# A two-layer encoder kernel: four modulation dots moved into attention, the first gate strip fetched between the value weights, and seven smaller edits of the order

## The chip, the cores and the metric

The kernel runs on one NeuronCore of a Trainium2 chip. The metric is the device time of one execution in microseconds, as the median of a few runs; lower is better. The core has a matrix engine (TensorE, in the profile PE, its weight loads PEld) and four others: VectorE (DVE), ScalarE (ACT), GpSimd (POOL) and SyncE (SP). Each engine works through its own list of instructions in order, and waits on semaphores where an instruction needs what another engine or a transfer has not delivered. In this kernel all transfers are issued by SP, so they form one more list that is worked through in order ("SPq").

## The reference

1024 tokens of width 1024 pass through two layers. Each layer is a root-mean-square norm with a shift and a scale that come from a conditioning vector c, a token mixer, a SiLU gate, an output projection and a gated residual add; a last norm closes the trunk.

```python
def _modulation(c, ada_w, ada_b):
    mod = jax.nn.silu(c) @ ada_w + ada_b
    shift, scale, gate = jnp.split(mod[:, None, :], 3, axis=-1)

for i in range(DEPTH):                                  # two layers
    shift, scale, gate = _modulation(c, ada_w[i], ada_b[i])
    h = _rmsnorm(x, norm_g[i]) * (1.0 + scale) + shift
    y = _diff_attention(h, ...) if i == 0 else _mla(h, ...)
    x = x + gate * y
return _rmsnorm(x, final_norm_g)

def _diff_attention(...):                               # layer 0, 8 heads, q and k of 2 x 64, v of 128
    q, k, v, z = jnp.split(h @ w_in, ...)               # rope on q and k
    p = jax.nn.softmax(sc, axis=-1)
    p = p[:, :, 0] - lam * p[:, :, 1]                   # difference of two softmaxes
    o = _rmsnorm(p @ v, subln_g) * (1.0 - lambda_init)
    return (o * jax.nn.silu(z)) @ w_out
```

Layer 1 is multi-head latent attention: one input projection to a low-rank query, a latent key/value, one rope key and the gate, then expansion to 8 heads, softmax, and the same gate and output projection.

## The kernel before, in words

**Precision.** Every large product is made of three matmuls on a high and a low part (`mm3`, L182 to L184: high·high, high·low, low·high). A part is made by a cast on ACT (high) and a subtraction on DVE or POOL (low). PE therefore has some 7,350 matmuls in one fixed order, and the program is a question of having the parts ready in time.

**Layer 0, first pass.** The tokens are taken in two halves of 512. For each of eight blocks of 128 features `h_chunk` transposes the tokens (L468), scales and shifts them (high part on ACT L473, the full value on DVE L477 or ACT L475) and subtracts (L478). With them PE makes the values of the first four heads (`vacc`), and, from weight strips, the keys and queries of head 0 (`acc`). A strip is 1024 x 128 weights for one head and one of k, q and z (z is the gate's input): two loads of 256 KB into `wraw` (L206, two buffers), a cast (L227), a subtraction (L228).

**V phase.** Then follow eight tiles `vps` of 28 or more matmuls (`v0_tile`): the values of the other four heads, one tile of 128 tokens each, from eight row blocks of weights `wv1[k]`. A block is loaded into `wvr` (L524, two buffers), cast (L533, ACT) and subtracted (L534, DVE); the subtraction is what frees the buffer for the next load. The first three blocks (`WV1` = 3) are loaded early, the other five behind `store_v`'s last cast. The first gate strip `z0raw` is fetched and used after the tiles have begun. Between the tiles run the streamed strips of the next heads and rope (transfers `rp_sw` L323).

**Modulation dots.** Layer 1's shift and scale need 16 dots `mod_dot` (L424, DVE, 128 x 1024): each needs a block of 512 KB that `mod_load` fetches (L419) and multiplies it with silu(c), with the sum along each row. Six stand in the second half of the first pass (k = 1 to 6), ten in the V phase (`MODS` = 2, 3, 3, 2 per tile). Layer 0's gate has eight more, made during attention 0 by `gate_steps0`, a generator that takes one step per query tile: load ahead, two steps, dot, two steps, dot.

**Attention 0.** For each head and query tile: scores (L850), row maximum (L400 DVE), exponential (L402 ACT), the two softmaxes combined (`e`, L858 DVE), four transposes (L383), a cast (`pth` L385 ACT) and a subtraction (`ptl` L386 DVE), the product with the values. A list of side tasks (`side`) is moved on by one entry at each tick; strips, rope, stacking of q (`qa`, `qb`, L352 to L358) and the row scales `bc_s` (L410) hang on it. The last head's task list of q holds as many empty ticks as the others'.

**Output projection.** `Seven` and `Pre7` make it of seven half-size products instead of eight. `Pre7` does the first products inside attention 0 and copies its sums out of the accumulators (`done`, L1264) when the next product begins.

**Transition.** The last products are added to the residual (`add0`, L1398), `group0` normalises four token tiles (reciprocal root on POOL L169, scaling of x on DVE L457 and ACT L455, tiles 1 and 3 on ACT) and begins layer 1's first pass with `h_chunk`.

**Layer 1 and tail.** `gate_steps` loads c again for its gate (L1858) and takes silu by a tanh (L1863). In the tail the sum is added (L2181), squared (L2187) and the norm applied (L2215 DVE, L2222 ACT). The reciprocal root is taken by `rsqrt8k`, seven small DVE instructions (L175 to L178), for tiles 4 to 6, and by a power on POOL (L169, then L2202) for the last.

## Time and profile before

| | us |
|---|---|
| runs | 1412.28, 1413.26, 1415.67 (median 1413.26) |
| profiled execution, its own time | 1415.68 |
| its span, first to last instruction | 1414.0 |
| PE busy in it | 1379.2 (98%) |
| DVE, ACT, POOL busy | 939.8, 737.5, 752.8 |

The profiled execution is 2.4 us above the median and as long as the slowest run; 1.7 us of it lie outside the span. PE is idle for 1414.0 - 1379.2 = 34.8 us of it. Reading the views: a row of the timeline is "start, duration, engine, line, operation, output<-inputs, shapes, count", and in square brackets how long the engine had been idle before and what ended that. "SPq" rows are transfers as issued. The view of windows gives, for each stretch, the busy time and count of each engine, then the granted clock of PE (1.00 is full), the share of time that the DMA engines were busy, and GB/s.

### The profile page before, as it was taken

To read this page: it belongs to the slowest core of one execution; us is meant where nothing else is said; L and a number is where in the kernel's file an instruction comes from. 1 tells how busy PE (TensorE), PEld (TensorE's weight loads), DVE (VectorE), ACT (ScalarE), POOL (GpSimd) and SP (SyncE) were. 2 spreads that over 40 slices of the span, in tenths; PEclk is the share of its full clock that TensorE was granted. 3 is DMA by queue.
4 is the path that set the end of the run, shared out by engine and by line. 5 is a ranking of instruction groups with operands and counts; after the bars stand their busy time and mean duration, and the time that the engine had idled before them with its cause. 6 is when DMAs were issued, how large, how long until landed. Compare 5 with 4: busy or idle time off the path is not lost.

```text
span 1414.0 us, 20751 instructions
## 1 busy us (share of the span) xinstructions
PE 1379.2 (98%) x7350; PEld 1150.3 (81%) x7350; DVE 939.8 (66%) x1339; ACT 737.5 (52%) x1331; POOL 752.8 (53%) x590
## 2 busy tenths in 40 slices
PE   8999999999999999999998999999999999999997
PEld 6778888888888888887786788887888888888886
DVE  7655677776666666668597885645666555555685
ACT  5532465565555556567646443335445454455554
POOL 4425274758686858675794323533141255653773
PEclk8999999999999999999999999999999999999999
DMA  9867634343444434526554136398533355566463
GB/s 336 260 201 235 201 92 131 99 139 99 149 111 151 127 120 127 154 56 209 180 216 164 39 104 217 128 314 237 173 108 117 102 165 176 194 207 218 142 233 120
DMA packets 149066, 231.54 MB, mean 164 GB/s; under 512 B 20577, under 2 KB 57569, under 8 KB 148962
## 3 DMA queue, kind: packets, MB, share of 16 engines
q1 hardware_dynamic: 148962, 230.21, 52.0%
q8 instruction: 58, 0.95, 0.3%
q14 instruction: 46, 0.38, 0.1%
HBM read 144.74 MB, written 61.81 MB: 146 GB/s over the span
## 4 chain that ended last, share of the span: by engine, by line
PE 78%; DVE 8%; DMA 4%; POOL 4%; ACT 3%; issue 2%; SPq 1%; POOLq 0%; DVEq 0%; ACTq 0%
PE s L2001 10%; PE acc L184 8%; PE acc L182 8%; PE acc L183 8%; PE tr L383 7%; PE s L850 6%; PE pv L184 4%; PE pv L182 4%; PE pv L183 4%; PE vps L183 1%; PE vps L184 1%; PE vps L182 1%; PE zacc L184 1%; PE zacc L183 1%; PE zacc L182 1%
## 5 line engine op out<-in xcount | busy, mean ns | idle before, releaser
L385 ACT CAST pth<-tr 128x512 fp32r<-128x512 f32 x256 | 150.1, 586 | 291.2 <-PE tr L383 289.4
L400 DVE TENSOR_REDUCE nm<-s 128x1 f32<-128x1024 f32 x192 | 234.1, 1219 | 86.5 <-PE s L850 76.5
L386 DVE TENSOR_TENSOR ptl<-tr,pth 128x512 fp32r<-128x512 f32 x256 | 176.3, 689 | 152.7 <-ACT pth L385 152.0
L228 POOL TENSOR_TENSOR wl<-wraw,wh 128x512 fp32r<-128x512 f32 (+2 forms) x79 | 101.1, 1283 | 187.9 <-ACT wh L227 169.1
L383 PE MATMUL tr<-ident,e 128*128 128x128 f32 x1024 | 155.5, 274 | 5.3 <-DVE ptl L386 5.1
L383 PEld LDWEIGHTS tr<-ident,e 128*128 128x128 f32 x1024 | 121.0, 140 | 48.4 <-DVE ptl L386 24.8
L402 ACT ACTIVATE e<-s,nm 128x1024 f32<-128x1024 f32 x128 | 143.5, 1121 | 26.0 <-DVE nm L400 23.3
L182 PE MATMUL acc<-h0h,wh 128*128 128x512 f32 x360 | 151.4, 421 | 0.0
L182 PE MATMUL pv<-pth,vt 128*128 128x256 f32 x512 | 147.2, 287 | 0.0
L183 PE MATMUL pv<-ptl,vt 128*128 128x256 f32 x512 | 145.4, 284 | 0.0
L184 PE MATMUL pv<-pth,vt 128*128 128x256 f32 x512 | 144.6, 282 | 0.0
L184 PE MATMUL acc<-h0h,wl 128*128 128x512 f32 x360 | 143.5, 399 | 0.0
L183 PE MATMUL acc<-h0l,wh 128*128 128x512 f32 x360 | 142.7, 396 | 0.0
L324 POOL TENSOR_TENSOR rp_r<-rp_raw,cosT 128x512 f32<-128x512 f32 x38 | 49.6, 1306 | 103.7 <-ACT rp_raw L319 53.3
L183 PEld LDWEIGHTS pv<-ptl,vt 128*128 128x128 f32 x512 | 97.6, 191 | 3.0
L182 PEld LDWEIGHTS pv<-pth,vt 128*128 128x128 f32 x512 | 97.4, 190 | 2.9
L184 PEld LDWEIGHTS pv<-pth,vt 128*128 128x128 f32 x512 | 97.6, 191 | 0.0
L1177 POOL TENSOR_TENSOR wol<-wol,woh 128x512 fp32r<-128x512 f32 x56 | 82.1, 1488 | 22.4 <-ACT woh L1176 19.8
L850 PE MATMUL s<-ks,qa 128*128 128x512 f32 x256 | 83.0, 405 | 4.5 <-DVE e L858 2.7
L329 POOL TENSOR_TENSOR rp_sw<-rp_sw,sinT 128x512 f32<-128x512 f32 x42 | 56.4, 1343 | 55.4 <-DMA rp_sw<-rp_raw 54.6
L858 DVE SCALAR_TENSOR_TENSOR e<-s,z,e 128x1024 f32<-128x1024 f32 x64 | 82.2, 1284 | 2.2
L850 PE MATMUL s<-ks,qb 128*128 128x512 f32 x256 | 80.2, 394 | 1.5 <-DMA qb<-qb 1.5
(412 smaller groups left out, 3488.8 us busy)
## 6 DMA issues: line engine op xcount, KB each, us to landing
ada<-in_ada_ss SPq DMA_DIRECT2D x32, 512.0 KB, 5.8
wraw<-in_w_s SPq DMA_DIRECT2D x64, 256.0 KB, 2.9
vS<-v_hl SPq DMA_DIRECT2D x32, 512.0 KB, 6.2
vt<-vS SPq DMA_DIRECT2D x32, 512.0 KB, 4.8
wol<-tS SPq DMA_DIRECT2D x56, 256.0 KB, 5.0
tS<-ob SPq DMA_DIRECT2D x48, 256.0 KB, 2.0
rp_sw<-rp_raw SPq DMA_DIRECT2D x168, 64.0 KB, 2.0
bc_s<-bc_d SPq DMA_DIRECT2D x34, 256.0 KB, 4.0
```

Of the source, the lines that this page charges most:

```text
L182: PE.matmul(psum, ah, bh, start=first, stop=False, skip_group_check=skip)
L183: PE.matmul(psum, ah, bl, start=False, stop=False, skip_group_check=skip)
L184: mm3.last = PE.matmul(psum, al, bh, start=False, stop=last, skip_group_check=skip).ins
L228: sub = (V if pair_of else G).tensor_sub(l_[:, :n], raw[:, :n], f32v(h_[:, :n]))
L383: transpose_p.last = PE.transpose(tr[:, j, :], p[:, kt * P : (kt + 1) * P], ident).ins
L385: mk["S"] = S.copy(pth[kh][:, :, dst], tr).ins
L386: mk["V"] = V.tensor_sub(ptl[kh][:, :, dst], tr, f32v(pth[kh][:, :, dst])).ins
L400: mk["V"] = V.reduce_max(nm, s_ps, axis=AX.X, negate=True).ins
L402: mk["S"] = S.activation(e, s_ps, AF.Exp, bias=nm, scale=1.0, accum_out=zs).ins
L850: PE.matmul(s_ps[:, kc * HF : (kc + 1) * HF], src[:, c, ql], KS[h][kc][:, c, :], start=fst, stop=not fst)
L858: combined.append(V.scalar_tensor_tensor(out=e0, in0=e1, scalar=z1[:, 0:1], in1=e0, op0=ALU.mult, op1=ALU.add).ins)
L2001: PE.matmul(s_ps[:, kc * HF : (kc + 1) * HF], lhs, rhs(kc), start=i == 0, stop=i == 4)
```

## The change

Nine edits, none of which changes what is computed but for the last bits of the tail's reciprocal root:

1. Layer 1's modulation dots are spread anew: four (not six) in the first pass, eight (not ten) in the V phase, and the last four in attention 0, in one query tile each, ahead of the gate's eight. The gate's dots then have one and two steps between them by turns, so that the sixteen steps stay sixteen.
2. The fetch of the first gate strip stands after the last modulation load of the first pass, between the value weights 0 to 2 and the rest. The order of PE follows: the gate strip's 48 matmuls now come ahead of the first `vps` tile.
3. Head 7 has one empty tick less ahead of stacking q.
4. `Pre7.done` is called with the eighth product, not with the next one.
5. `group0`'s first group scales x tile 2 on ACT as well, and makes the full value of chunks 0 and 2 on ACT; in the seventh product the first two token tiles are worked by turns and added together.
6. One more v tile of layer 1 stands ahead of its first scores (`V1_AT`).
7. Layer 1's gate loads c two ticks later, and its tanh comes one tick later than before.
8. `DEF1` gives way to one empty tick for the first half of heads 1 to 7.
9. `rsqrt8k` is gone; tiles 4 to 6 of the tail take POOL's power like the last one.

```diff
@@ -37,14 +37,14 @@
     NVEC += _c
 DEF = 7
 ROT = 3
-DEF1 = 0
...
 Z_PRE = 16
 V_LATE = 6
-MODS = (2, 3, 3, 2, 0, 0, 0, 0)
-V1_AT = (3, 2)
+MODS = (2, 2, 2, 2, 0, 0, 0, 0)
+MODS_K = 4
+V1_AT = (3, 3)
 NORM_AT = 5
 PRE0 = (0, 0, 0, 0, 1, 2, 2, 3, 2, 2, 2)
 PRE1 = (0, 0, 0, 0, 0, 0, 0, 1, 1, 1, 1)
@@ -169,15 +169,6 @@
-    def rsqrt8k(w):
-
-        y, u = sm.tile([P, 1], F32, name="rq_y"), sm.tile([P, 1], F32, name="rq_t")
-        V.tensor_scalar(y.bitcast(I32), w.bitcast(I32), -0.5, float(0x5F3759DF), op0=ALU.mult, op1=ALU.add)
-        for c in (3.0, 12.0, 768.0):
-            V.tensor_scalar(u, w, y[:, 0:1], y[:, 0:1], op0=ALU.mult, op1=ALU.mult)
-            V.scalar_tensor_tensor(out=y, in0=u, scalar=-c, in1=y, op0=ALU.add, op1=ALU.mult)
-        return y
-
@@ -431,15 +422,19 @@
         mod_dot(ws[1], bsc[:, js], a_[:, js], c_)
         return V.scalar_tensor_tensor(out=a_[:, js], in0=a_[:, js], scalar=1.0, in1=g[:, js], op0=ALU.add, op1=ALU.mult).ins
 
+    def mod_job(n):
+
+        j, i = divmod(n, 2)
+        _, bsh, bsc, a_, b_ = mods[1]
+        bias, acc = ((bsh, b_), (bsc, a_))[i]
+        return A["ada_ss1"][j, i], bias[:, j : j + 1], acc[:, j : j + 1]
+
     def gen_mods(load, c2):
 
-        g, bsh, bsc, a_, b_ = mods[1]
-        for j in range(KT):
-            for i, (bias, acc) in enumerate(((bsh, b_), (bsc, a_))):
-                mod_dot(load(A["ada_ss1"][j, i]), bias[:, j : j + 1], acc[:, j : j + 1], c2)
-                if j == KT - 1 and i == 1:
-                    V.scalar_tensor_tensor(out=a_, in0=a_, scalar=1.0, in1=g, op0=ALU.add, op1=ALU.mult)
-                yield
+        for n in range(sum(MODS) + MODS_K):
+            src, bias, acc = mod_job(n)
+            mod_dot(load(src), bias, acc, c2)
+            yield
 
 
     def inv_rms(ss, n):
@@ -721,7 +716,7 @@
     vacc = [bank("acc", "vacc") for _ in range(4)]
...
-            if 0 < k < 7:
+            if 0 < k <= MODS_K:
                 next(mods_g)
@@ -775,7 +770,7 @@
 
             r = []
             sum_ = [lambda: r.append(fin()), None] if 0 < h < 5 else []
-            side.add(*[None] * ROT, rot, *[None] * (DEF - 1 - ROT), *sum_, g)
+            side.add(*[None] * ROT, rot, *[None] * (DEF - 1 - ROT - (h == NH - 1)), *sum_, g)
         return f
 
     def silu_gate(tp, acc):
@@ -798,12 +793,12 @@
     for h in range(NH):
         items += [(strip0(1, h), h0, k_done(h)), (strip0(0, h), h0, q_done(h)), (strip0(2, h), h0, z_done(h))]
     wv1 = [load_wv(A["w_v0"][k, 1], V) for k in range(WV1)]
+    with tc.issue_after(mod_load.last):
+        z0raw = fetch_strip([A["w_s0"][2, 0, f] for f in range(2)], [4, 4])
     with tc.issue_after(store_v.act):
         wv1 += [load_wv(A["w_v0"][k, 1], V) for k in range(WV1, KT)]
     with tc.issue_after(h_last):
         k_done(0)(kacc, 0)
-    with tc.issue_after(mod_load.last):
-        z0raw = fetch_strip([A["w_s0"][2, 0, f] for f in range(2)], [4, 4])
     for _ in gen_half(wk0, h0, 1, lambda acc: k_done(0)(acc, 1)):
         pass
     wz0 = split_strip(z0raw)
@@ -1057,15 +1052,21 @@
         gcol = sm.tile([P, KT], F32, name="gcol", tag="gcol", bufs=1)
         yield
         w = []
-        for j in range(KT):
-            while len(w) < min(2, KT - j):
+        jobs = [mod_job(n) for n in range(sum(MODS) + MODS_K, 2 * KT)]
+        late = len(jobs)
+        jobs += [(A["ada_g0"][j], part("ada_bg0")[:, j : j + 1], gcol[:, j : j + 1]) for j in range(KT)]
+        for n in range(len(jobs)):
+            while len(w) < min(2, len(jobs) - n):
                 with tc.issue_after(mod_load.last):
-                    w.append(mod_load(A["ada_g0"][j + len(w)], pg, 2))
+                    w.append(mod_load(jobs[n + len(w)][0], pg, 2))
             yield
-            yield
-            js = slice(j, j + 1)
+            if n >= late and (n - late) % 2 == 0:
+                yield
             with behind("V"):
-                mod_dot(w.pop(0), part("ada_bg0")[:, js], gcol[:, js], c2)
+                mod_dot(w.pop(0), *jobs[n][1:], c2)
+                if n == late - 1:
+                    g, _, _, a_, _ = mods[1]
+                    V.scalar_tensor_tensor(out=a_, in0=a_, scalar=1.0, in1=g, op0=ALU.add, op1=ALU.mult)
         SP.dma_start(gateS[0].rearrange("(p j) -> p j", p=P), gcol)
         yield
         SP.dma_start(c2, gateS[0][None, :].to_broadcast([P, D]))
@@ -1221,13 +1222,13 @@
                 self.n += 1
                 return self.step()
             if not h and not i:
-                if n:
-                    self.done(self.accs)
                 self.accs = [bank("acc", "oy") for _ in range(2)]
                 ssq_at.append(self.accs[1])
             with tc.issue_after(transpose_p.last):
                 self.sv.mm(n, self.accs[i], h, i, start=True)
             self.n += 1
+            if self.n == 8:
+                self.done(self.accs)
 
     stX, stO = ExitStack(), ExitStack()
     xp = None
@@ -1404,7 +1405,7 @@
     def group0(gi):
         fulls = [[x_] for x_ in xf[4 * gi : 4 * gi + 4]]
         V.tensor_add(ssa[gi], ssa[gi], ssb[gi])
-        norm_x(ssa[gi], fulls, (2, 3) if gi else (1, 3))
+        norm_x(ssa[gi], fulls, (2, 3) if gi else (1, 2, 3))
 
         def chunk(k):
             if gi == 1:
@@ -1412,7 +1413,7 @@
                 h1f[k] = ut(f"h1f{k}", dt=F32)
             else:
                 h1[k][0] = [h1p.tile([P, HF], F32R, name="h1_" + x_, tag="h1", bufs=16) for x_ in "hl"]
-            lm["V"] = h_chunk(1, fulls, k, h1[k][gi], p3x, V, f32=h1f[k] if gi else None)
+            lm["V"] = h_chunk(1, fulls, k, h1[k][gi], p3x, V, act=not gi and k in (0, 2), f32=h1f[k] if gi else None)
             if gi == 0:
                 lm["h"] = h_chunk.act
 
@@ -1482,11 +1483,15 @@
                 sv0.fetch_w(6, h)
             w6 = sv0.last
         for i in range(4):
-            for h in range(4):
-                sv0.mm(n, acc[i], h, i, start=n == 3)
-                if n > 4 and ((4 * i + h) % 3 == 2 if n == 5 else h % 2):
+            order = [(i, h) for h in range(4)]
+            if n == 6 and i < 2:
+                order = [(j, 2 * i + h) for h in range(2) for j in range(2)]
+            for c, (j, h) in enumerate(order):
+                sv0.mm(n, acc[j], h, j, start=n == 3)
+                if n > 4 and ((4 * i + c) % 3 == 2 if n == 5 else c % 2):
                     side.tick()
-            add0(rows + i, acc[i], f, n == 4 or n > 4)
+            for j in (i,) if n < 6 or i > 1 else range(2) if i else ():
+                add0(rows + j, acc[j], f, n > 3)
             if n == 4:
                 SP.dma_start(x1S[i][:, halves[0]], xf[i][:, halves[0]])
                 junk = p3.tile([P, HF], BF16, name="tjunk", tag="tjunk", bufs=1)
@@ -1854,9 +1859,10 @@
 
     def gate_steps():
 
+        yield
+        yield
         for i in range(2):
             SP.dma_start(cg2[i], A["c"][:, i * HF : i * HF + HF].to_broadcast([P, HF]))
-        yield
         yield
         for i in range(2):
             with behind("S"):
@@ -1962,7 +1968,7 @@
                 stack_q(qa, qb, fin())
                 QP.setdefault(h, [None, None])[half] = qa, qb
 
-            side.add(None, rot, *[None] * DEF1)
+            side.add(None, rot, *[None] * (h > 0 and not half))
             if h and half:
                 late_q.append(g)
             elif half:
@@ -2197,12 +2203,10 @@
             V.scalar_tensor_tensor(out=w, in0=ss, scalar=1.0 / D, in1=w, op0=ALU.mult, op1=ALU.add)
         if not final:
             return add.ins
-        if tt == NT - 1:
+        if early:
             y = rsqrt(w, 1)
             G.tensor_scalar(y, y, -8192.0, None, op0=ALU.mult)
             scale(tt, y[:, 0:1])
-        elif early:
-            scale(tt, rsqrt8k(w)[:, 0:1])
         elif tt == 3:
             y4.append(rsqrt(w4, 4))
             G.tensor_scalar(y4[0], y4[0], -8192.0, None, op0=ALU.mult)
```

The orders below are the lists of instructions, in the order of each engine; "x2" counts equal neighbours. The first place is DVE at the end of the first pass, where `ada,c` are the modulation dots, `v_hl` the values' low parts and `wvl` the weights' low parts. Before:

```order
99 L363 TENSOR_TENSOR v_hl<-vacc,v_hl 128x512 x3
100 L424 ISA ada,modb_105<-ada,c_202,vec 128x1024
101 L424 ISA modb_105 128x1
102 L363 TENSOR_TENSOR v_hl<-vacc,v_hl 128x512
103 L424 ISA ada,moda_104<-ada,c_202,vec 128x1024
104 L424 ISA moda_104 128x1
105 L534 TENSOR_TENSOR wvl<-wvr,wvh 128x512 x2
106 L324 TENSOR_TENSOR rp_r<-rp_raw,cosT 128x512
107 L534 TENSOR_TENSOR wvl<-wvr,wvh 128x512 x4
```

and with the change:

```order
99 L354 TENSOR_TENSOR v_hl<-vacc,v_hl 128x512 x4
100 L529 TENSOR_TENSOR wvl<-wvr,wvh 128x512
101 L315 TENSOR_TENSOR rp_r<-rp_raw,cosT 128x512
102 L529 TENSOR_TENSOR wvl<-wvr,wvh 128x512 x3
103 L315 TENSOR_TENSOR rp_r<-rp_raw,cosT 128x512
104 L529 TENSOR_TENSOR wvl<-wvr,wvh 128x512 x2
```

The dots 5 and 6 are gone from between the values and the weights, and all four `v_hl` stand ahead of them.

The second place is SP at the same point, where `wvr` are the value weights, `wraw` the gate strip, `ada` the dots' blocks and `vS` the stored values. Before:

```order
40 L524 DMA wvr<-in_w_v 128x512 x2
41 L419 DMA ada<-in_ada_ss 128x1024 x2
42 L524 DMA wvr<-in_w_v 128x512 x2
43 L419 DMA ada<-in_ada_ss 128x1024 x2
44 L365 DMA vS_0_77<-v_hl 256x4x128 x4
45 L524 DMA wvr<-in_w_v 128x512 x2
46 L323 DMA rp_sw<-rp_raw 32x512 x3
47 L524 DMA wvr<-in_w_v 128x512 x2
48 L323 DMA rp_sw<-rp_raw 32x512
49 L206 DMA wraw<-in_w_s 128x512 x2
```

and with the change:

```order
40 L519 DMA wvr<-in_w_v 128x512 x2
41 L410 DMA ada<-in_ada_ss 128x1024 x2
42 L519 DMA wvr<-in_w_v 128x512
43 L197 DMA wraw<-in_w_s 128x512 x2
44 L519 DMA wvr<-in_w_v 128x512
45 L314 DMA rp_sw<-rp_raw 32x512
46 L356 DMA vS_0_77<-v_hl 256x4x128 x4
47 L519 DMA wvr<-in_w_v 128x512 x2
48 L314 DMA rp_sw<-rp_raw 32x512 x3
49 L519 DMA wvr<-in_w_v 128x512 x2
```

The gate strip (`wraw`) went up from behind the eighth value weight to between the third and the fourth, and two blocks of dots left this place.

The third is ACT at the transition, where L455 (with the change L450) scales x, L473 (L468) makes the high part of a chunk of h, and L470 of the change is the full value on ACT; ahead of both pieces stands the scaling of tile x_1. Before:

```order
564 L455 ACTIVATE x_3_7172<-x_3_7172,rq_y 128x1024
565 L1402 ACTIVATE tjunk,ss_7180<-x_4_7173 128x512
566 L1176 CAST woh<-wol 128x512
567 L1402 ACTIVATE tjunk,ss_7180<-x_5_7174 128x512
568 L1176 CAST woh<-wol 128x512
569 L227 CAST wh<-wraw 128x512 x3
570 L1402 ACTIVATE tjunk,ss_7180<-x_6_7175 128x512
571 L227 CAST wh<-wraw 128x512
572 L1402 ACTIVATE tjunk,ss_7180<-x_7_7176 128x512
573 L473 ACTIVATE h_h<-trh,modb_105,moda_104 128x512 x2
```

and with the change:

```order
564 L450 ACTIVATE x_2_7171<-x_2_7171,rq_y 128x1024
565 L450 ACTIVATE x_3_7172<-x_3_7172,rq_y 128x1024
566 L1403 ACTIVATE tjunk,ss_7180<-x_4_7173 128x512
567 L1177 CAST woh<-wol 128x512
568 L1403 ACTIVATE tjunk,ss_7180<-x_5_7174 128x512
569 L1177 CAST woh<-wol 128x512
570 L218 CAST wh<-wraw 128x512
571 L1403 ACTIVATE tjunk,ss_7180<-x_6_7175 128x512
572 L218 CAST wh<-wraw 128x512 x3
573 L1403 ACTIVATE tjunk,ss_7180<-x_7_7176 128x512
574 L468 ACTIVATE h_h<-trh,modb_105,moda_104 128x512
575 L470 ACTIVATE h_7774<-trh,modb_105,moda_104 128x512
```

ACT scales one tile more (x_2) ahead of the next `tjunk`, and chunk 0's full value (`h_7774`) came to it from DVE, as chunk 2's does later.

## The prediction

> **What bounds the kernel now.** I read the page's first part, then the gaps of PE in the timeline, the windows around the costliest, and the chain of waits there.
>
> ```profile
> span 1414.0 us, 20751 instructions
> PE 1379.2 (98%) x7350; PEld 1150.3 (81%) x7350; DVE 939.8 (66%) x1339; ACT 737.5 (52%) x1331; POOL 752.8 (53%) x590
> ```
>
> PE is busy for 1379.2 of 1414.0 us, so an edit that removes no matmul can win at most the 34.8 us in which PE idles, and what it loses at a lower clock. The change keeps the matmuls. So the question for each edit is whether it closes or opens a gap of PE. The costliest place is the start of the V phase:
>
> ```profile
> 97.10:100.50 3.40, 2.00 (x7) 0.78 (x5) 1.54 (x2) 1.73 (x3) 1.05 (x1) 1.00 0.77 228
> 100.50:104.00 3.50, 2.70 (x7) 2.17 (x7) 2.68 (x4) 2.02 (x4) 2.18 (x3) 0.50 0.53 170
> 104.00:107.40 3.40, 3.40 (x9) 2.67 (x8) 0.00 (x0) 1.43 (x3) 3.25 (x3) 0.51 0.25 62
> 98.83 0.73 PE L182 MATMUL vps<-wvh,h0h 128*128 128x512 f32 x2 [1.41 <-ACT wvh L533]
> 101.34 0.80 PE L183 MATMUL vps<-wvl,h0h 128*128 128x512 f32 x1 [0.80 <-DVE wvl L534]
> ```
>
> PE waits 1.41 us for a weight's cast and 0.80 us for its subtraction, and then works at a granted clock of 0.50 for two windows. In these it is busy 2.70 + 3.40 = 6.1 us, half of which is lost: 3.05 us. The chain says why the weight is late:
>
> ```profile
> 88.66 5.50 DMA wvr<-in_w_v
> 94.18 1.24 ACT wvh L533 x2
> 95.44 0.70 DVE wvl L534
> 96.16 2.81 DMA wvr<-in_w_v
> 99.00 0.63 ACT wvh L533
> 99.65 1.64 DVE wvl L534
> 101.34 0.80 PE vps L183
> ```
>
> There are two buffers, so each pair of loads (5.50 and 2.81 us) waits until the pair before it is cast and subtracted, and the matmul waits for the last of these. Ahead of the first pair, DVE had worked off a modulation dot (next fence).
>
> **Term A, the V phase's weights (edits 1 and 2).** Two things change here. First, the sixth dot goes:
>
> ```profile
> 86.74 1.28 DVE L424 CUSTOM_DVE_ANT_0 ada<-ada,c,vec 128x1024 f32<-128x1024 f32 x1 [1.75 <-DMA ada<-in_ada_ss]
> 81.95 6.17 SPq L365 DMA_DIRECT2D vS<-v_hl  x4
> 88.66 1.43 SPq L524 DMA_DIRECT2D wvr<-in_w_v  x2
> ```
>
> The subtractions that free the first pair's buffers stand on DVE behind it, and with it go 1.75 us of waiting and 1.28 of work on DVE, but SP issues the four stores `vS` until 81.95 + 6.17 = 88.12, and the third pair of weights stands behind them. So the loads start only some 0.5 us sooner, unless the stores also move up. This alone would not close 1.41 + 0.80. Second, the gate strip's 48 matmuls now run ahead of the tile. PE reaches the `vps` tile at 93.1 us before, ten matmuls after the first of these rows, so a matmul takes (93.14 - 90.80)/10 = 0.23 us:
>
> ```profile
> 90.80 0.40 PE L184 MATMUL acc<-h0h,wl 128*128 128x512 f32 x1
> 93.14 0.40 PE L182 MATMUL vps<-wvh,h0h 128*128 128x512 f32 x1
> ```
>
> With the change it does at 93.1 + 48 x 0.23 = 104.2, and asks for weight 6, 18 matmuls on, at 108.3. By the chain, shifted by the 0.5 us, weight 6 is there by 99 and weight 7 by 101: 7 us to spare. The gate strip itself must then be ready at 93.1. Its two cast tiles take the buffers of head 0's k strip, whose second half ends at 90.80 + 0.40, and with the change six matmuls sooner (the last six of q follow it), at 89.8. A cast and a subtraction later:
>
> ```profile
> L228 POOL TENSOR_TENSOR wl<-wraw,wh 128x512 fp32r<-128x512 f32 (+2 forms) x79 | 101.1, 1283 | 187.9 <-ACT wh L227 169.1
> ```
>
> 0.6 (as for `wvh` above) + 1.28 gives 91.7 for the second tile, wanted after 12 matmuls at 93.1 + 2.8 = 95.9; the first tile is 12 matmuls (2.8 us) ahead in both. So both are in time by some 4 us, and the strip's load is not late: it now stands two value weights earlier on SP. So the two waits vanish (2.2 us), and with them, I think, the slow stretch: together -5.3, with bounds 0 and -5.3. What was behind the stall comes 5 us sooner, so what could be late next are the streamed strips; they have room, as PE has no wait at all from 110 to 300 us:
>
> ```profile
> 110.00:160.00 50.00, 50.00 (x224) 41.40 (x223) 30.58 (x47) 13.90 (x23) 16.29 (x10) 1.00 0.84 262
> 160.00:300.00 140.00, 140.00 (x779) 119.03 (x778) 105.52 (x151) 85.33 (x151) 82.10 (x65) 1.00 0.42 119
> ```
>
> On the clock: the half clock here, from the window at 100.50 on, followed an idle 1.41 us and began together with the second wait of 0.80. The Trainium skill, page "TensorE: Matmul & The Clock Gate", section "Why this matters for your kernels", asks for no idle gap over about 3 us. The measurement disagrees, since 1.41 us was enough here; and yet a stretch with 1.59 us of idle time in one piece (at 754 us, quoted in term D) kept the full clock:
>
> ```profile
> 754.40:757.40 3.00, 1.41 (x7) 1.19 (x7) 3.00 (x5) 2.52 (x5) 0.45 (x2) 1.00 0.68 263
> ```
>
> So an idle time of this length does not decide it alone, and I keep a rival for that.
>
> **Term G, four dots in attention 0.** The eight there now:
>
> ```profile
> L424 DVE CUSTOM_DVE_ANT_0 ada<-ada,c,vec 128x1024 f32<-128x1024 f32 x8 | 11.9, 1483 | 0.0
> DVE z L856 <- ACT s L402: 5.5, 7, 2.0
> ```
>
> None waited for its block, and they take 1.48 us each; four more are 5.9 us of DVE, which is busy 105.5 of 140 us there. Each stands ahead of `z`, which otherwise waits for ACT's exponential, and PE has other work (the strips) meanwhile. The price is 0, with 4 x 1.48 = 5.9 as the bound if all came onto PE's path; below nothing is excluded, since PE does not wait there. The cover gone, DVE's next row maximum would be late, and with it the exponential and the transposes. The V phase loses two dots, in a place without waits: 0.
>
> **Term B, head 7's q (edit 3).**
>
> ```profile
> 624.61 0.33 SPq L410 DMA_DIRECT2D bc_s<-bc_d  x1
> 626.28 0.54 SPq L357 DMA_DIRECT2D qa<-qa  x1
> 629.13 0.70 PE L850 MATMUL s<-ks,qa 128*128 128x512 f32 x2 [1.35 <-DMA qa<-qa]
> ```
>
> PE waits 1.35 us for q, issued behind a row scale and two rope transfers (between the first two rows). With one tick less, three of its four transfers go ahead of them, so q is up to 626.28 - 624.61 = 1.7 us sooner, if ACT's casts come sooner as well. I take -0.9; bounds 0 and -1.35.
>
> **Term C, end of attention 0 (edit 4).**
>
> ```profile
> 687.05 1.07 ACT L1264 COPY p<-oy 128x512 f32<-128x512 f32 x2
> 687.42 0.55 PE L383 MATMUL tr<-ident,e 128*128 128x128 f32 x3 [1.46 <-DVE ptl L386]
> ```
>
> Three of the last four transposes wait 1.46 us for the accumulator that `ptl` frees; with the change six `oy` matmuls (6 x 0.23 = 1.4 us) stand ahead of them. -1.2; bounds 0 (if the six wait for their own weights' cast on ACT instead) and -1.46.
>
> **Term D, transition (edit 5).**
>
> ```profile
> 751.77 3.48 DVE L457 TENSOR_SCALAR x<-x,rq_y 128x1024 f32<-128x1024 f32 x2 [1.19 <-POOL rq_y L169]
> 753.22 2.18 ACT L455 ACTIVATE x<-x,rq_y 128x1024 f32<-128x1024 f32 x2
> 755.99 0.47 PE L182 MATMUL oy<-woh,oah 128*128 128x512 f32 x1 [1.59 <-DVE x L1398]
> 763.13 0.66 PE L468 MATMUL trh<-ident,x 128*128 128x128 f32 x4 [0.74 <-DVE h L477]
> ```
>
> DVE is rid of one scaling of two (3.48/2 = 1.74 us), so `add0`, for which PE waits 1.59, comes 1.7 us sooner; ACT gets 2.18/2 = 1.09 more, and its scaling of the last tile ends at 753.22 + 3 x 1.09 = 756.5, up to 0.7 us after the time PE asks for it. The chunks' full values go to ACT, so that DVE's 0.74 and a like one at chunk 2 turn into waits for ACT, which is later by 1.09 less what it gains from the earlier add. Gains 1.6 + 2 x 0.7, losses up to 0.7 + 2 x 1.1, about even; since the add's wait is sure to go and the losses are upper ends, I take -0.6, bounds -1.5 and +1.5.
>
> **Term E, layer 1's gate (edit 7).**
>
> ```profile
> 979.40 0.63 ACT L1863 ACTIVATE gwh<-c2h 128x512 f32<-128x512 f32 x1 [1.29 <-DMA c2h<-in_c]
> 981.28 0.66 PE L383 MATMUL tr<-ident,e 128*128 128x128 f32 x4 [1.07 <-DVE ptl L386]
> ```
>
> ACT waits 1.29 us for c; behind it stand `pth`, then `ptl`, for which PE waits 1.07. The loads come two ticks later, the tanh one: less time between them, but q and k no longer stand behind c on SP. The gap goes only if the tanh, too, finds other work ahead: -0.8; bounds -1.07 and, should ACT wait a whole transfer more, +1.3.
>
> **Term F, tail (edit 9).**
>
> ```profile
> 1406.66 0.58 POOL L169 TENSOR_TENSOR rq_y<-tw,mhalf 128x1 f32<-128x1 f32 x1 [9.47 <-DVE rq_y L178]
> 1407.33 0.24 POOL L2202 TENSOR_SCALAR rq_y<-rq_y 128x1 f32<-128x1 f32 x1
> 1408.27 0.15 DVE L178 SCALAR_TENSOR_TENSOR rq_y<-rq_t,rq_y 128x1 f32<-128x1 f32 x1
> 1410.02 0.41 SPq L2216 DMA_DIRECT2D out_y<-x  x1
> ```
>
> Tile 6's root came at 1408.27 from DVE; POOL takes 0.58 + 0.24 = 0.82 for it, but ACT's scaling of it now stands ahead of the last tile's square. +0.4; bounds -0.6 and +0.8. Edits 6 and 8 move tiles among work for which PE does not wait: 0.
>
> **Sum.** -5.3 - 0.9 - 1.2 - 0.6 - 0.8 + 0.4 = -8.4 against this execution's own 1415.7 (span 1414.0 and 1.7 around it): 1407.3. It is 2.4 above the median, and the three runs lie 3.4 apart, about one slow stretch. If the 2.4 are a general offset, 1413.3 - 8.4 = 1404.9. I forecast the middle, **1406.0**.
>
> **The rivals.** (1) The slow stretch is not the stall's doing, or comes elsewhere: 3.05 less, 1409.1. For it: the longer gap without one; against: it began within the stall. (2) ACT's chain in the transition makes one long wait (its third transposition, up to 3.3 us by my walk through the rows) which the clock answers with a slow stretch of 3.05, and term D is +1.5: 1406 + 2.1 + 3.05 = 1411.2. By the Trainium skill's rule named above a gap over 3 us would do it. (3) The dots in attention hold DVE: standing in four neighbouring tiles and then in pairs, they find their 512 KB blocks not landed; eight of the twelve then wait as the first pass's did (1.75), the row maxima behind them on DVE come late, and PE stands for scores: 8 x 1.75 = 14, 1420; it decides from 1.0 us a dot over the twelve, which makes 1418. Against: 0.0 us of waiting for the eight now, and DMA engines busy 0.42 of the time there. (4) The change does not do what it says: the gate strip waits for its buffers or load by as much as the weights did, A = 0: 1411.3.
>
> **Chances.** Forecast 0.55 (own range 1402 to 1409), (1) 0.17, (2) 0.08, (3) 0.12, (4) 0.08. A measurement of this kernel tells about 0.3% from no change, 4.2 us: below 1409.0 is faster, above 1417.5 slower. Faster takes 0.54 of the forecast and about half of (1) and a little of (2) and (4): 0.66; slower is nearly all of (3): 0.11; the rest 0.23. The range's low end is the lower footing 1404.9 with B to F at their better bounds (-0.45, -0.26, -0.9, -0.27, -1.0) and 0.5 for the runs: 1401.5. Its high end reaches over (1), (2) and (4): 1411.3 with D at +1.5 (2.1 more) and half the runs' spread, 1.7, is 1415. It leaves out (3).
>
> **What would show it.** A: no wait of PE above 0.3 us from 85 to 115 and the clock at 1.00 there. B, C, E: no row of L850, L383 with over 0.5 us of idle time at these places. D: the wait of 1.59 gone and none over 1 us for ACT in its place. G: the twelve dots with idle 0.0 ahead, and PE 100% busy in 160 to 300. F: the last issue of `out_y` comes 1410.02 - 1406.66 = 3.4 us after the last power begins, give or take 0.8, with tile 6's root ready before it. I am wrong if one of the windows turns slow, or if dots wait for their blocks.

## The result, and the profile after

The changed kernel takes 1405.02 us (median of 6 runs, 1404.0 to 1408.36) against 1413.32 for the kernel before (6 runs, 1412.28 to 1415.67): a ratio of 0.9941, 95% interval 0.9930 to 0.9952, or 8.3 us less. The forecast was 1406.0, in a range of 1401.5 to 1415. It was faster, and by the amount that was forecast; but two terms of the sum (the transition, layer 1's gate) came out by another way or with the other sign, and PE also works on the same matmuls in less time, for which the sum has no term. Two executions far off the others, one of 2751.6 us with layer 1's gate undone and one of 1507.3 us with the strip's casts held back, count in the medians of those two kernels below and not in their ratios.

The page of the changed kernel's profiled execution, its first lines:

```profile
span 1402.2 us, 20727 instructions
PE 1373.1 (98%) x7350; PEld 1148.8 (82%) x7350; DVE 937.0 (67%) x1315; ACT 739.5 (53%) x1334; POOL 754.2 (54%) x596
```

The span is 11.8 us shorter than before (1414.0), more than the 8.3 of the medians. PE has as many matmuls and is busy 6.1 us less. Matched matmul by matmul, 3.6 us of that lie between 60 and 112 us, where the slow stretch of 3.05 us is gone; 2.3 lie between 112 and 600 us and 1.3 between 800 and 950 us, where the clock is full in both kernels. The windows of the changed kernel at the start of the V phase (length, then busy time and count of PE, PEld, DVE, ACT, POOL; granted clock, DMA share, GB/s):

```profile
93.40:96.80 3.40, 3.40 (x16) 2.81 (x16) 2.84 (x3) 0.97 (x2) 1.60 (x1) 1.00 0.70 192
96.80:100.20 3.40, 3.40 (x16) 2.82 (x16) 2.10 (x4) 1.76 (x3) 0.46 (x1) 1.00 0.27 78
100.20:103.60 3.40, 3.40 (x16) 2.81 (x16) 1.30 (x4) 1.26 (x3) 3.25 (x3) 1.00 0.32 77
```

PE is busy throughout and the clock is 1.00: the waits of 1.41 and 0.80 us and the slow stretch are gone, as term A said. The transition, in windows and then in the timeline of PE and ACT, is less kind:

```profile
747.30:750.70 3.40, 0.93 (x5) 0.41 (x3) 0.00 (x0) 3.40 (x9) 3.40 (x4) 1.00 0.17 34
750.70:754.10 3.40, 2.93 (x9) 2.55 (x10) 2.92 (x4) 2.53 (x4) 2.67 (x2) 0.50 0.69 228
```

```profile
740.98 3.23 ACT L450 ACTIVATE x<-x,rq_y 128x1024 f32<-128x1024 f32 x3
746.37 0.62 ACT L218 CAST wh<-wraw 128x512 fp32r<-128x512 f32 x1
747.52 1.64 ACT L218 CAST wh<-wraw 128x512 fp32r<-128x512 f32 x3
749.69 0.76 ACT L468 ACTIVATE h_h<-trh,modb,moda 128x512 fp32r<-128x512 f32 x1
751.17 1.11 PE L463 MATMUL trh<-ident,x 128*128 128x128 f32 x4 [2.94 <-ACT h L470]
```

The wait of 1.59 us for the adds has become one of 2.94 us for ACT, with a window at clock 0.50 behind it. ACT is busy 3.40 of 3.40 us while PE waits, with scalings, squares and the next strip's casts (L218) ahead of the chunk. And layer 1 has a wait that was not there before:

```profile
965.83 0.87 SPq L1865 DMA_DIRECT2D c2h<-in_c  x2
966.75 0.90 SPq L365 DMA_DIRECT2D vt<-vS  x2
973.16 0.39 PE L173 MATMUL pv<-pth,vt 128*128 128x256 f32 x1 [1.87 <-DMA vt<-vS]
```

The two kernels have 7350 matmul records each, so the start of the k-th matmul can be compared between the traces. By that measure the changed kernel is ahead by 0.9 us when the first pass is under way (its start-up lost less to a half clock), by 6.8 at 107 us, by 9.1 at 612, 11.5 when attention 0 ends, 12.0 after the transition, at 800, 13.1 at 965, 12.2 at 986, and 11.2 at PE's last matmul; the end adds 0.6 (times of the kernel before). The start-up is not of the change: over all thirteen profiles of changed kernels here the 62nd matmul starts between 19.8 and 21.0 us.

### The profile page after: what moved, and what is told of

Its sections match the earlier page's. It is cut to its first block, busy times and chain, and to the rows that moved or that the text cites. A ratio compares the mean times of both kernels' runs of the same rounds, so it can differ in the third digit from the quotient of the medians.

```text
span 1402.2 us, 20727 instructions
## 1 busy us (share of the span) xinstructions
PE 1373.1 (98%) x7350; PEld 1148.8 (82%) x7350; DVE 937.0 (67%) x1315; ACT 739.5 (53%) x1334; POOL 754.2 (54%) x596
## 4 chain that ended last, share of the span: by engine, by line
PE 80%; DVE 6%; POOL 4%; DMA 4%; ACT 3%; issue 2%; SPq 1%; POOLq 0%; DVEq 0%; ACTq 0%
PE s L2007 10%; PE acc L173 8%; PE acc L175 8%; PE acc L174 8%; PE tr L374 7%; PE s L845 7%; PE pv L173 4%; PE pv L175 4%; PE pv L174 4%; PE oy L174 2%; PE oy L173 2%; PE oy L175 2%; PE vps L173 2%; PE vps L174 2%; PE vps L175 2%
## 5 line engine op out<-in xcount | busy, mean ns | idle before, releaser
L175 PEld LDWEIGHTS acc<-h0h,wl 128*128 128x128 f32 x360 | 67.5, 188 | 15.1
```

The costliest lines, as they stand in the source:

```text
L175: mm3.last = PE.matmul(psum, al, bh, start=False, stop=last, skip_group_check=skip).ins
```

## The experiments

Each kernel is the changed one with the edit shown, but for the last. Ratios are to the kernel before, run on the same chip beside it; the intervals are 0.0011 to 0.0016 wide to each side, 1.5 to 2.2 us.

| | median us | ratio (95%) |
|---|---|---|
| changed, again | 1406.73 | 0.9950 (0.9938 to 0.9963) |
| strip's fetch undone | 1407.89 | 0.9960 (0.9948 to 0.9973) |
| dots undone | 1412.89 | 0.9994 (0.9983 to 1.0005) |
| dots halfway | 1407.20 | 0.9954 (0.9942 to 0.9966) |
| full values back on DVE | 1405.73 | 0.9949 (0.9936 to 0.9962) |
| third scaling undone | 1406.55 | 0.9952 (0.9940 to 0.9963) |
| strip's casts held back | 1404.64 | 0.9933 (0.9920 to 0.9946) |
| layer 1's gate undone | 1407.73 | 0.9955 (0.9942 to 0.9967) |
| v tile undone | 1404.84 | 0.9942 (0.9928 to 0.9956) |
| edits 3, 4 and 9 undone | 1408.76 | 0.9966 (0.9954 to 0.9979) |
| two mends together | 1405.25 | 0.9943 (0.9930 to 0.9955) |
| edits 1 and 2 alone | 1408.88 | 0.9961 (0.9945 to 0.9976) |

### The changed kernel again

> The changed kernel once more, as the yardstick for the three beside it: 1405.0 us, give or take 1.5. In the two profiles at hand PE of the changed kernel drew ahead by another 2.3 us between 107 and 560 us, where neither kernel waits. If that belongs to the change (fewer dots in the V phase, say), it shows here again; if it is the difference of one execution from the next, this profile lies up to 2 us away from the other one of the same kernel over that stretch.

1406.73. Its profile starts 0.8 us later than the other one of this kernel and is within 0.2 us of it from 757 us. The expectation's own test speaks for the change: from 107 to 560 us this profile draws ahead of the kernel before by another 2.35 us, the other one by 2.4. That neither kernel waits there does not hold, but they wait alike: PE idles for 4.2 us of it in the kernel before and for 4.1 and 3.7 in the two profiles of this one. What differs is how long PE works on the same matmuls; the run with edits 3, 4 and 9 undone comes back to that.

The kernels below that are edited only at 600 us or later, whose program is the same up to there, are 1.2 to 2.9 us behind the other profile at 560 us, this one 0.6, in part by waits of their own (1.32 us at 136 us in the one with the third scaling undone). So a single profile is a poor yardstick for an effect of 2 us.

### The gate strip and the dots (edits 1 and 2)

The strip's fetch in its old place:

```diff
-    with tc.issue_after(mod_load.last):
-        z0raw = fetch_strip([A["w_s0"][2, 0, f] for f in range(2)], [4, 4])
     with tc.issue_after(store_v.act):
         wv1 += [load_wv(A["w_v0"][k, 1], V) for k in range(WV1, KT)]
     with tc.issue_after(h_last):
         k_done(0)(kacc, 0)
+    with tc.issue_after(mod_load.last):
+        z0raw = fetch_strip([A["w_s0"][2, 0, f] for f in range(2)], [4, 4])
```

> Only the gate strip's place is undone (edit 2); the dots stay moved. Theory (two buffers, so the weights come in pairs 5.5 and 2.8 us apart, and only other matmuls can cover that): the vps tile again waits, by 2.2 us less the 0.5 that the loads start sooner, about 1.7 us in one or two pieces, and a slow stretch may follow: 1406.7 without it, 1409.8 with it. Rival (the dot that waited for its block was what made the weights late): no wait over 0.3 us there, 1405.0.

Neither. The order of instructions shows what the expectation missed: with the dots moved, the planner that lays out PE's order puts only 5 matmuls of the tile ahead of the strip's 48 even with the fetch in its old place (28 before, none in the changed kernel). The timeline of this kernel:

```profile
81.12 4.30 SPq L356 DMA_DIRECT2D vS<-v_hl  x4
85.51 2.99 SPq L519 DMA_DIRECT2D wvr<-in_w_v  x2
94.32 0.50 PE L173 MATMUL acc<-h0h,wh 128*128 128x512 f32 x1 [0.86 <-ACT wh L218]
95.68 0.50 PE L175 MATMUL acc<-h0h,wl 128*128 128x512 f32 x1 [0.39 <-POOL wl L219]
```

PE waits 1.25 us, now for the strip, and no slow stretch follows. The value weights are not late at all, because the four stores end at 85.4 us and the loads behind them start at 85.5, where before they started at 88.66: 3.2 us sooner, 2.2 when the lead from the start-up is taken off. The stores waited for `v_hl` on DVE, which stood between the dots.

The dots in their old places, the strip's fetch in its new one:

```diff
-MODS = (2, 2, 2, 2, 0, 0, 0, 0)
-MODS_K = 4
+MODS = (2, 3, 3, 2, 0, 0, 0, 0)
+MODS_K = 6
...
+            if n == 2 * KT - 1:
+                g, _, _, a_, _ = mods[1]
+                V.scalar_tensor_tensor(out=a_, in0=a_, scalar=1.0, in1=g, op0=ALU.add, op1=ALU.mult)
...
-            if n >= late and (n - late) % 2 == 0:
+            if n >= late and (not late or (n - late) % 2 == 0):
```

> Only the dots' places are undone (edit 1: six in the first pass, ten in the V phase, none of layer 1's in attention 0); the gate strip stays ahead of the vps tile. Theory (the strip's 48 matmuls cover the loads with 7 us to spare): no wait at the start of the V phase, and nothing is won or lost by the four dots: 1405.0, give or take 0.7. Rival (moving the dots does the work): the weights are late by a part of the old 2.2 us, 1406 to 1409. A third (the dots in attention cost something): faster than 1404.

All of the gain is gone, 1412.89. Here too the planner lays out another order: 2 matmuls of the tile, 24 of the strip, 5 of the tile, then the strip's other 24, and PE waits 1.12 and 0.49 us ahead of the strip's two halves, at 94 and 102 us. The larger loss is later. The timeline in the V phase, on DVE and PE:

```profile
141.33 1.28 DVE L415 CUSTOM_DVE_ANT_0 ada<-ada,c,vec 128x1024 f32<-128x1024 f32 x1 [3.80 <-DMA ada<-in_ada_ss]
147.49 0.50 PE L173 MATMUL vps<-wvh,h0h 128*128 128x512 f32 x1 [0.93 <-DVE v_hl L354]
151.86 1.27 DVE L415 CUSTOM_DVE_ANT_0 ada<-ada,c,vec 128x1024 f32<-128x1024 f32 x1
154.30 1.22 DVE L391 TENSOR_REDUCE nm<-s 128x1 f32<-128x1024 f32 x1
158.73 0.71 PE L848 MATMUL s<-ks,qa 128*128 128x512 f32 x2 [2.63 <-DVE e L856]
```

A dot waits 3.80 us for its block, and what stands behind it on DVE (`v_hl`, then the first row maxima of attention) comes late by that; PE waits 0.93 and 2.63 us, and the window after that, from 160.1 us, has the clock at 0.51. This is the mechanism that the third rival had placed in attention 0; it sat in the V phase. The kernel before had ten dots there too and no such wait. Its last pair of blocks, and its last dot, came sooner, as its timeline shows ahead of the same row of this kernel:

```profile
137.60 1.56 SPq L419 DMA_DIRECT2D ada<-in_ada_ss  x2
146.46 1.27 DVE L424 CUSTOM_DVE_ANT_0 ada<-ada,c,vec 128x1024 f32<-128x1024 f32 x1
```

```profile
142.65 2.37 SPq L410 DMA_DIRECT2D ada<-in_ada_ss  x2
```

The load is issued 5.1 us later and the dot comes 5.4 later (151.86), while PE, without the old stall, stands ready for the scores at 156.1; the last matmul ahead of them comes 1.7 us sooner than in the kernel before. Why SP comes to the blocks later in this order was not tried by itself.

Halfway, with six dots in the first pass, eight in the V phase and two in attention 0:

```diff
-MODS_K = 4
+MODS_K = 6
```

> The dots halfway: six in the first pass as before, two per tile in the V phase and two in attention 0; the gate strip ahead of the vps tile. The run with all dots put back lost 6 us, with waits at 94 us (1.1: the strip's load stands behind the last dot's block and the stores) and at 146 and 156 us (0.9 and 2.6, with a slow stretch). Theory (two separate places, each with its own dots): only the wait at 94 us comes back, 1406 to 1407, and PE does not wait at 146 or 156. Rival (the first pass's late weights run on into the V phase): waits of 2 us or more at 146 to 156 as well, 1410 or more.

As the theory had it, 1407.20. PE waits at 94 us (its order there is that of the run before), and the largest wait from 146 to 156 us is 0.49 us. Two rows of this kernel:

```profile
87.82 2.04 SPq L197 DMA_DIRECT2D wraw<-in_w_s  x2
94.09 0.50 PE L173 MATMUL acc<-h0h,wh 128*128 128x512 f32 x1 [1.25 <-ACT rp_raw L310]
```

The strip's load, bound to stand behind the last dot's, comes after the stores; ACT can cast it only at 92.94, and the copy `rp_raw`, for which PE waits, stands behind that cast. Compared with the run before, the two dots less in the V phase are worth 5.7 us of the medians (1412.89 to 1407.20), and the two less in the first pass 0.5 to 2.2 (to 1406.73 and 1405.02).

### The transition (edit 5)

The full values of chunks 0 and 2 on DVE again:

```diff
-            lm["V"] = h_chunk(1, fulls, k, h1[k][gi], p3x, V, act=not gi and k in (0, 2), f32=h1f[k] if gi else None)
+            lm["V"] = h_chunk(1, fulls, k, h1[k][gi], p3x, V, f32=h1f[k] if gi else None)
```

> In the transition the full values of chunks 0 and 2 go back to DVE; ACT keeps the scaling of x tile 2. Theory (the 2.94 us for which PE waits there is ACT's chain of tjunk, casts, the high part and the full value, and the slow stretch of 3.4 us comes from that one long wait): the wait falls to waits under 1 us each for DVE and the clock stays full: 2.9 + 1.7 less about 1.6 of new waits, 1402.0. Rival (ACT is held by the third scaling, so the high part alone is late as well): the wait stays over 2 us, 1405.0.

The rival's case: 1405.73, and PE still waits over 3 us, as this kernel's timeline shows. ACT reaches the first chunk's high part 1.5 us after PE has come to a stop at 750.2.

```profile
751.67 1.43 ACT L468 ACTIVATE h_h<-trh,modb,moda 128x512 fp32r<-128x512 f32 x2
753.33 0.90 PE L463 MATMUL trh<-ident,x 128*128 128x128 f32 x3 [3.13 <-DVE h L472]
```

The third scaling undone:

```diff
-        norm_x(ssa[gi], fulls, (2, 3) if gi else (1, 2, 3))
+        norm_x(ssa[gi], fulls, (2, 3) if gi else (1, 3))
```

> In the transition x tile 2 is scaled on DVE again, as before; all else as in the changed kernel. Theory (ACT's queue is the long one there, so that moving 1.09 us more onto it bought nothing): PE waits 1.6 us for the adds again but less than 2 us for the first chunk's high part, and the sum of both is what the changed kernel waits in one piece (2.4 to 2.9): 1405, or 1.7 less where no slow stretch follows. Rival (the third scaling was worth its 1.6 us): 1406.5.

1406.55. The timeline of PE shows two waits where the changed kernel has one:

```profile
747.33 0.47 PE L173 MATMUL oy<-woh,oah 128*128 128x512 f32 x1 [1.74 <-DVE x L1399]
754.29 0.66 PE L463 MATMUL trh<-ident,x 128*128 128x128 f32 x4 [1.67 <-ACT h L470]
```

Together 3.41 against 2.94 us, and no slow stretch, since neither fills enough of a window. So taking 1.74 us off DVE bought less than half a microsecond of waiting; ACT was the next in line. The time is the rival's, 1406.5, though the waits are the theory's: this profile also has the wait at 136 us that the edit does not reach. The medians can't tell these kernels apart.

The casts of the next strip held back behind the first chunk:

```diff
             if i > 1 and n == 6:
-                w4.append(split_strip(raws.pop(0), h1p if i == 3 else None))
+                with tc.issue_after(lm["h"]):
+                    w4.append(split_strip(raws.pop(0), h1p if i == 3 else None))
```

> In the transition the four casts of layer 1's first strip are held back behind the first chunk's high part on ACT (some 2.2 us of ACT's work move behind it); all else as in the changed kernel. Putting the chunks' full values back on DVE had left the wait of 3.1 us, and ACT came to the first chunk only 1.5 us after PE stood. Theory (ACT's queue of scalings, squares and casts is the long one there): the wait at 749 us falls from 2.4 to 3.1 us to under 1 us and no slow stretch follows, 2 + 1.7 less: 1402. Rival (the wait only moves: the strip's matmuls after the chunks now wait for their late casts and POOL's four subtractions of 1.3 us): 1405 or more, with a wait of PE at 770 to 780 us.

PE's waits in the transition:

```profile
749.67 0.66 PE L463 MATMUL trh<-ident,x 128*128 128x128 f32 x4 [0.45 <-ACT h L470]
766.59 0.33 PE L463 MATMUL trh<-ident,x 128*128 128x128 f32 x1 [0.61 <-DVE x L452]
768.26 0.55 PE L463 MATMUL trh<-ident,x 128*128 128x128 f32 x3 [1.34 <-DVE x L452]
```

The long wait is 0.45 us, so ACT's queue was its cause. But 17 us later PE waits 1.95 us for the second group's scaling on DVE. Matched by matmuls, this kernel gains 4.0 us on the other profile by 752 us, that one's slow stretch included, and has 2.3 of them left at 780; 1.9 more go at 970 us, where it waits 2.29 us for `vt` and a slow stretch follows. 1404.64 is the lowest ratio of all, 0.9933, and is not apart from the changed kernel's by its interval.

### Layer 1's gate and the v tile (edits 7 and 6)

c loaded at once, its tanh one tick sooner:

```diff
-        yield
-        yield
         for i in range(2):
             SP.dma_start(cg2[i], A["c"][:, i * HF : i * HF + HF].to_broadcast([P, HF]))
         yield
+        yield
```

> Only edit 7 is undone: c is loaded at once and its tanh comes one tick sooner again. The changed kernel waits 1.1 to 1.9 us at 971 us for the values vt, a wait that the kernel before did not have. Theory (the loads of c now stand directly ahead of vt on SP and share its transfer time): that wait goes, and the old 1.07 us behind the tanh comes back: no net difference, 1405. Rival (the v tile put ahead of the scores makes vt late): the wait for vt stays, and the old one comes on top: 1406.

The wait for `vt` goes, as the theory had it, and the old one comes back larger. From this kernel's timeline:

```profile
960.76 2.92 SPq L1863 DMA_DIRECT2D c2h<-in_c  x2
968.55 0.63 ACT L1868 ACTIVATE gwh<-c2h 128x512 f32<-128x512 f32 x1 [2.86 <-DMA c2h<-in_c]
970.43 1.12 PE L374 MATMUL tr<-ident,e 128*128 128x128 f32 x4 [2.64 <-DVE ptl L377]
```

From issue to use c takes 7.8 us, though it is 256 KB a piece. PE reaches this place 12.5 us sooner than in the kernel before by the matched traces, but c is used only 10.9 us sooner (968.55 against 979.40), and so PE waits 2.64 instead of 1.07.

One v tile fewer ahead of the scores:

```diff
-V1_AT = (3, 3)
+V1_AT = (3, 2)
```

> Only edit 6 is undone: one v tile fewer ahead of layer 1's first scores. Theory (c's loads make vt late): the wait for vt at 971 us stays at 1 to 2 us, 1405. Rival (the v tile does it): the wait goes and the end comes 1 to 2 us sooner, 1403.5.

The wait for `vt` stays, 1.95 us, and 1404.84 is the same as with the edit: the v tile did not cause it, and is worth nothing that can be measured.

### Edits 3, 4 and 9

The definition of `rsqrt8k` comes back too; it stands in the diff of the change.

```diff
-            side.add(*[None] * ROT, rot, *[None] * (DEF - 1 - ROT - (h == NH - 1)), *sum_, g)
+            side.add(*[None] * ROT, rot, *[None] * (DEF - 1 - ROT), *sum_, g)
...
             if not h and not i:
+                if n:
+                    self.done(self.accs)
...
             self.n += 1
-            if self.n == 8:
-                self.done(self.accs)
...
-        if early:
+        if tt == NT - 1:
             y = rsqrt(w, 1)
...
+        elif early:
+            scale(tt, rsqrt8k(w)[:, 0:1])
```

> Three small edits undone that lie far apart, so that each is read at its own place: head 7's q (edit 3), Pre7.done (edit 4), the tail's power on POOL (edit 9). Theory, from comparing the two profiles matmul by matmul: edit 3 is worth 1.5 us (the wait of 1.35 for q at 619 us comes back), edit 4 1.2 (the wait of 1.46 at 675 us), edit 9 0 to 0.6 in the time from PE's last matmul to the end: together 2.7 to 3.3 us slower, 1408 to 1409. Rival (each wait is only handed on to the next): one or both of the waits come back but PE has made it up 20 us later, 1405 to 1406.5.

Both waits come back in the timeline of PE, and the one of the transition is smaller:

```profile
622.01 0.70 PE L854 MATMUL s<-ks,qa 128*128 128x512 f32 x2 [1.15 <-DMA qa<-qa]
680.07 0.55 PE L383 MATMUL tr<-ident,e 128*128 128x128 f32 x3 [1.45 <-DVE ptl L386]
753.46 0.66 PE L472 MATMUL trh<-ident,x 128*128 128x128 f32 x4 [1.36 <-ACT h L479]
```

For the waits, theory and rival both hold: by the matched matmuls the two edits are worth 1.2 and 0.9 us at their places, but PE, arriving later, waits 1.36 instead of 2.94 in the transition and not at all for `vt`. From 60 us on it idles for 14.4 us here, for 16.5 in the changed kernel, and no slow stretch follows the transition. By its waits this kernel would be the faster one. It is not: 1405.3 in this execution against 1404.0, and the median of six, 1408.76, is 2 to 3.7 us above the two medians of the changed kernel.

What the waits leave over is the time that PE takes for the same work. From its 4100th to its 4740th matmul the order is the same in all fourteen profiles, PE idles for 0.15 us at most, and the clock is full. Windows of 138 us from the 4100th on, of the kernel before, of this kernel, and of the changed kernel run again:

```profile
810.10:948.10 138.00, 138.00 (x635) 114.16 (x634) 89.82 (x119) 54.10 (x97) 53.98 (x40) 1.00 0.56 182
800.00:938.00 138.00, 137.98 (x634) 113.79 (x633) 89.45 (x119) 53.92 (x96) 54.53 (x40) 1.00 0.58 181
798.10:936.10 138.00, 138.00 (x642) 115.29 (x641) 89.59 (x120) 54.45 (x97) 55.04 (x41) 1.00 0.58 184
```

Such a window holds 634 or 635 matmuls in the three profiles without edits 3, 4 and 9 (these two and edits 1 and 2 alone), and 640 to 642 in the eleven with them. From the 661st to the 3077th matmul, 160 to 600 us, it is the same: PE is busy for 435.8 to 436.2 us in the three and for 433.4 to 434.1 in the eleven. The two stretches together make 3.3 us between the two profiles of before and after. Up to 611 us every engine has the same instructions in the same order in this kernel and the changed one, so the first of these gains can't come from a change of order. Edit 9 also takes a tile, `rq_t`, out of the program; whether that is the reason was not tried by itself, and the cause stays open.

From PE's last matmul to the end it takes 8.2, 8.4 and 8.9 us in the three kernels with the small DVE steps and 8.3 to 9.0 in those with POOL's power: at the tail, edit 9 can't be told from nothing.

### Two mends together

```diff
-        yield
-        yield
         for i in range(2):
             SP.dma_start(cg2[i], A["c"][:, i * HF : i * HF + HF].to_broadcast([P, HF]))
         yield
+        yield
+        yield
...
-                w4.append(split_strip(raws.pop(0), h1p if i == 3 else None))
+                with tc.issue_after(lm["h"]):
+                    w4.append(split_strip(raws.pop(0), h1p if i == 3 else None))
```

> Two additions to the changed kernel: the four casts of layer 1's first strip held behind the first chunk on ACT (as tried), and c's loads for layer 1's gate at their old early place with the tanh left at its new late one. Theory (c's loads take about 8 us from issue to use and must be ahead of vt on SP by that much; the tanh must not be reached sooner): the wait for vt at 970 us (1.1 to 2.3, sometimes with a slow stretch of 1.7) and the wait at 967 us both go, and the one at 749 us is gone as tried: 1405.0 less 1.5 to 2 for each place, 1402. Rival (the vt transfers are late anyway, because of the stores ahead of them): a wait of over 1 us stays at 970 us, 1404.

The waits for `vt` and for the tanh are gone, and 1405.25 is no gain. PE waits 1.18 us for layer 1's q instead, which now stands behind c on SP, and 0.58 and 1.34 at 767 us, here with a slow stretch:

```profile
767.05 0.33 PE L463 MATMUL trh<-ident,x 128*128 128x128 f32 x1 [0.58 <-DVE x L452]
768.72 0.55 PE L463 MATMUL trh<-ident,x 128*128 128x128 f32 x3 [1.34 <-DVE x L452]
970.10 0.73 PE L2008 MATMUL s<-kps,qpa 128*128 128x512 f32 x2 [1.18 <-DMA qpa<-qpa]
```

### Edits 1 and 2 alone

The kernel before with `MODS`, `MODS_K`, `mod_job`, the new `gate_steps0` and the strip's fetch, and nothing else of the change.

> The kernel before with edits 1 and 2 alone (dots moved, gate strip ahead); all seven others undone. Theory (term A, the weights' stall and the slow stretch behind it, is most of the gain; the other edits' gains largely hand their waits on): PE does not wait at 93 to 101 us, the clock is full there, and the kernel is 5.3 us faster than before, 1408.0, while the seven others are worth the 1.5 to 3 us that are left. Rival (the other edits' prices add up as forecast, 3.1 us, or more, since moving the dots also relieves later places): 1410 or 1406. In this kernel the waits before q of head 7 (1.35 us), at the end of attention 0 (1.46) and before the adds (1.6) should be there again.

1408.88, ratio 0.9961: 5.5 us less than before (3.4 to 7.8), where the theory said 5.3. This kernel's windows at the V phase, and the wait at the end of attention 0 from its timeline:

```profile
93.40:96.80 3.40, 3.40 (x16) 2.81 (x15) 2.21 (x3) 1.24 (x2) 0.87 (x1) 1.00 0.64 198
96.80:100.20 3.40, 3.40 (x16) 2.81 (x16) 2.74 (x6) 1.24 (x2) 1.40 (x2) 1.00 0.36 86
```

```profile
681.50 0.55 PE L383 MATMUL tr<-ident,e 128*128 128x128 f32 x3 [1.46 <-DVE ptl L386]
```

No stall and the full clock in the V phase; the waits of the later edits are all there again (1.20 us for q, 1.46 here, 1.59 for the adds). The seven other edits together are worth the difference to the changed kernel, 2 to 4 us by its two medians. Little of that is waiting: between the two profiles PE's idle time from 60 us on falls from 17.8 to 16.5 us, a slow stretch comes in, and PE's last matmul is still 5.3 us sooner, 3.9 of it in the two stretches described above (436.19 against 433.62 us, and 139.58 against 138.25). Edit 8 and the seventh product's order were not undone by themselves.

## Why the prediction was right, and where it was not

| term | forecast | measured |
|---|---|---|
| A, start of the V phase | -5.3 | -6.0 in the matched traces, -5.5 with edits 1 and 2 alone |
| G, dots in attention 0 | 0 | 0 |
| B, head 7's q | -0.9 | -1.4 |
| C, end of attention 0 | -1.2 | -0.9 |
| D, transition | -0.6 | -0.5 |
| E, layer 1's gate | -0.8 | +0.9 |
| F, tail | +0.4 | -0.6 in the profile, not apart from 0 |

The measured terms add up to -8.5, the forecast ones to -8.4, and the medians differ by 8.3; that is closer than the working deserves. The two profiles differ by 11.8 us. Of the rest, 3.2 us were won where no term stands (112 to 612 and 800 to 965 us), for the most part in the time for the same matmuls, 0.9 at the start, and 1.0 was lost behind 986 us; and the profile of before is the longest of its six runs, that of after the shortest. That so near a hit came out of it is partly luck.

**A** was right in size, and the slow stretch belonged to the stall, against the first rival: it is gone from this place in every kernel here, in those that keep a shorter wait too, and in the one with edits 1 and 2 alone. The rival's other half, that one comes elsewhere, did happen, in the transition. But the working failed in the step "the loads start only some 0.5 us sooner, unless the stores also move up. This alone would not close 1.41 + 0.80". The stores did move up, since they waited for DVE behind the dots, and the loads with them, by 2.2 us. With the dots moved alone the weights are in time; what is then late is the strip. Nor are the edits separate: the dots decide, through the planner, where the strip's matmuls stand.

**G.** The twelve dots in attention 0 had no idle time ahead of them, and PE was busy 139.91 of 140 us from 160 to 300. The third rival fell there. But the step "the V phase loses two dots, in a place without waits: 0" failed: the place has no waits in the order of the kernel before. With the strip's fetch moved, two dots more in the V phase cost 5.7 us, as much as all of A; the strip's gain holds only with them gone.

**B and C** were right in mechanism: both waits are gone, for 1.4 and 0.9 us by the matched traces.

**D** went the second rival's way in part and came out as forecast by luck: over the seven profiles with this transition the lead grows by 0.1 to 1.7 us across it. The adds' 1.59 us were won; ACT's one long wait (2.94; the rival said up to 3.3) and a slow stretch took them back. By the prediction's own signs, no wait over 1 us for ACT and no window turned slow, D is refuted. The step that failed is "the chunks' full values go to ACT, so that DVE's 0.74 and a like one at chunk 2 turn into waits for ACT": the waits are not the full values' but those of the whole queue ahead of them, as the held-back casts showed.

**E** failed in the step "q and k no longer stand behind c on SP": true, but nothing was said of `vt`, which then stood right behind c. The wait went from one transfer's user to the next.

**F**'s sign was wrong by less than kernels differ in it. Its check missed, too: the last `out_y` is issued 2.1 us after the last power begins, not 3.4 give or take 0.8.

## What to carry to other kernels

Where one engine is 98% busy, a closed wait is worth its length only until the next thing that was hidden by it: here 5.5 us held, and most of the later, smaller ones were handed on to a scaling, a square or a load that nobody had waited for before. Ask of every operation that costs nothing now whether it still does in the new order, when the path comes sooner or its load later; the V phase's dots did not. And in an order that a planner lays out, an edit undone alone is not the sum's missing term: look at the order first. Before a gain is put down to waits, count the matmuls in a stretch without waits in both kernels: here the same ones took 0.5 to 0.8% less time in one of them, by a cause that is still open.
